# Low parts of weights made by adding transfers, S5 column groups in turn, gated parts one head behind

## The chip, the cores and the metric

One core of a Trainium2 chip runs the whole program. The metric is device time in microseconds for one execution. Three runs of the kernel before took 1574.0 to 1582.47 us, with a median of 1578.91 us. The page and the trace are of one profiled execution, which took 1579.79 us; its span, from the first to the last instruction, is 1577.7 us, so 2.1 us lie outside the span.

The engines by their names in the rows: PE is TensorE (PEld its weight loads), DVE VectorE, ACT ScalarE, POOL GpSimd, SP SyncE, which issues most transfers. GpSimd issues the others, among them those that add to what stands at the target.

## What is computed

A backbone of two layers over 1280 tokens (256 of context, 1024 latent) and 1024 channels. Layer 0 is the one that the change touches: a projection of the normed tokens, a gated linear recurrence (RG-LRU) of 8 heads in both directions, a diagonal state space model (S5) of 32 groups in both directions with a gated linear unit (GLU) behind it, a SiLU gate on each branch, and an output projection. Layer 1 is latent attention of 8 heads. Cut to layer 0:

```python
def rglru_coeffs(u, wr, br, wi, bi, lam):
    r = sigmoid(einsum('blhi,hij->blhj', uh, wr) + br)
    i = sigmoid(einsum('blhi,hij->blhj', uh, wi) + bi)
    log_a = -LRU_C * r * softplus(-lam)
    return exp(log_a), sqrt(-expm1(2.0 * log_a)) * (i * u)      # a, b of h = a h + b

def even_mix(h, ...):
    xa, ga, ub, gb = split(h @ w_in, EVEN_SPLITS, axis=-1)
    ya = rglru_mix(xa, ...)                                      # both directions, added
    yb = s5_mix(ub, ...)                                         # gelu(y) * sigmoid(gelu(y) @ glu_w + glu_b)
    return concatenate([ya * silu(ga), yb * silu(gb)], -1) @ w_out
```

## The kernel before

**High and low parts.** TensorE multiplies in a format shorter than fp32 (fp32r). To keep fp32's precision each operand is held as a rounded high part and the remainder as a low part, and each product is made of three matmuls (`mm3`, L209 to L211): high weight by high data, high weight by low data, low weight by high data. The parts of a weight are made by `split` (L178): ScalarE casts the raw tile to the high part (L182), VectorE subtracts it from the raw tile for the low part (L184). The parts of data are made in the same way by `split_big` (ScalarE L1196, VectorE L1198).

**Buffers.** Raw weights come to SBUF by `raw_weights` (L194, on SyncE's queue) into one buffer of the pool `wp`; high and low parts have two buffers each. Gate weights have two buffers of each kind in the pool `gw`.

**Order.** Layer 0's recurrences are issued in an order written out by hand. Three strings of turns (`TURNS`) name steps; turn n runs with one string, and a step's last character says how many heads it is behind. Turns 0 and 1 run with the first string (they also make the S5 weights, step E), turns 2 to 6 with the second, turn 7 with the third, which runs on into the GLU and the first tiles of the output projection. Each engine executes its instructions in this order and waits only for data and buffers. The second string, and the end of the third:

```python
    ("D01 H11 M11 k21 U1- Q11 a21 G000 l00 N01 P0 G100 s21 B11 r21 U0- d21 D11 N11 W0 P0 o21 l10 a00 "
     "k00 s00 P0 r00 d00 C1- W0 Y1 P0 G110 o00 k10 G010 a10 C0- s10 M00 V0- V1- C2- A10 r10 A00 H00 I- Q00 "
     "d10 P0 O- l20 P0 B00 o10").split(),
     "N00 X10 Z30 N10 J00 X00 X20 F30 X30 P0 Y0 P0 P0 S10 P0 S30 P0 F00 W0 P0 S00 K00 F50 S50 J10 P0 "
     "F40 F20 W0 P0 P0 S40 F70 K10 W0 J20 P0 P0 S20 P0 S70 P0 J30 P0 P0 K20 T10 W0 P0 T00 K30 P0 "
     "P0 F60 T20 W0 S60 T30").split())
```

The steps that matter here:
- U loads a raw gate weight (128x2x128), V makes its parts, G multiplies with it (four times per head, ScalarE's sigmoid at L917 behind each block).
- W makes the parts of the next weight tile and issues the load of the one after it; P multiplies one of the three token blocks (256, 512, 512 columns) of the current tile. The tiles in order: projections of gates and heads, 4 of the GLU (512 rows), 16 of the output projection (768 rows each).
- N are the scans of a head (L943, L947, L948); the first direction's result is stored by GpSimd (L945), the second one's is added to it in DRAM by an adding transfer of GpSimd (Y, L953).
- l, k, a, s, r, d, o are the steps of an S5 batch. In r VectorE scans (L1020, L1021), GpSimd sets two edges to zero (L1023, L1024), VectorE copies (L1025). In d VectorE makes the product that o's matmul L1040 reads.
- E is one step of `s5_weights`, which makes 8 K blocks: for each of four groups, matmuls of 128 columns (L526) and of 16 (L529) into 32 partitions of one PSUM bank; ScalarE copies the bank (L530), VectorE adds the skip term (L531).
- Z, X load and split the S5 output; F loads a head's mixed result and its gate, S multiplies them (L1136) and splits the product at once; K and T do the same for the S5 part with the GLU's result.

`store` sends finished rows from SyncE, in the order in which they were noted, at the next P, E, Z, F or o. `out0` runs the rest of the output projection: six P and two W for each pair of tiles, with `residual` (its store by GpSimd, L1230) behind every second tile.

Of the kernel before, what the change touches and what calls it, by code (L numbers as in the profile page):

```python
# [9 lines left out]
F32 = mybir.dt.float32  # L10
F32R = mybir.dt.float32r
AF = mybir.ActivationFunctionType
ALU = mybir.AluOpType
# [119 lines left out]
class Kernel:  # L133
# [63 lines left out]
    def weight_parts(self, raw):  # L197
        return self.split(raw, self.wp, "w", 2, list(raw.shape))

# [259 lines left out]
    def s5_weights(self, Pre, Pim, bb, ccp):  # L459
# [9 lines left out]
        for Q in range(8):  # L469
            gs = slice(4 * Q, 4 * Q + 4)  # L470
            if Q % 4 == 0:

                Kt = self.tl(sp, [128, 4, 144], "s5K", 1)
                pads = []
# [46 lines left out]
            for g4 in range(4):  # L521
                g = 4 * Q + g4
                o = pk[32 * g4:32 * g4 + 32]
                for k in range(2):
                    C = Cs[k][:, g4].rearrange("p m h -> p (m h)")
                    nc.tensor.matmul(o[:, 16:144], pads[k][:, g % 16], C[:, 16:144], start=(k == 0), stop=(k == 1))  # L526
                for k in range(2):
                    both = bb[:, k, g:g + 2].rearrange("p g h -> p (g h)")
                    nc.tensor.matmul(o[:, 0:16], both, Cs[k][:, g4, 0], start=(k == 0), stop=(k == 1))  # L529
# [358 lines left out]
    def recurrences(self, steps):  # L888
# [8 lines left out]
        class Head:  # L897
# [8 lines left out]
            def V(x, d):  # L906
                x.gw[d] = self.split(x.raw.pop(d), self.gp, "gw", 2, [128, 2, 128])
# [150 lines left out]
        class Tiles:  # L1058
# [3 lines left out]
            def load(x):  # L1062
                if x.n_raw < len(tiles):
                    kind, i, _ = tiles[x.n_raw]
                    src, k = {"glu": (t["glu_w"], 4), "out": (t["w_out"], 6)}.get(kind, (t["w_in"], 8))
                    src = src[i // 2, :, 6 * (i % 2):6 * (i % 2) + 6] if kind == "out" else src[i]
                    x.raws.append(self.raw_weights(src, k))
                    x.n_raw += 1

            def W(x):  # L1070
                if x.raws:
                    x.ws.append(self.weight_parts(x.raws.pop(0)))
                    x.load()

            def P(x):
# [7 lines left out]
                w = x.ws[0]  # L1083
                src = {"glu": lambda: x.y, "out": lambda: self.mix[6 * (i % 2):6 * (i % 2) + 6]}.get(kind, lambda: self.n0)()
# [24 lines left out]
            yg, y, g, gb, m, ga = {}, [None] * 4, {}, {}, {}, {}  # L1109
# [24 lines left out]
            def S(x, h):  # L1134
                m, g = x.m.pop(h), x.ga.pop(h)
                nc.vector.tensor_mul(m, m, g)  # L1136
                self.mix[h] = self.split_big(m, alloc=self.far)
# [697 lines left out]
```

## Time and profile before

| | before |
|---|---|
| median of 3 runs | 1578.91 us (1574.0 to 1582.47) |
| profiled execution | 1579.79 us, span 1577.7 us |
| busy in the span: TensorE, VectorE, ScalarE, GpSimd | 94%, 72%, 52%, 3% |
| transfers: SyncE's queue, GpSimd's queue (share of the 16 engines) | 32.3%, 7.6% |

The page divides the span into 40 slices of 39.4 us. A digit is the busy share of the slice in tenths, one line for each engine. Layer 0's recurrences lie between about 158 and 645 us, its output projection between 645 and 810 us, then come layer 1's projections and the attention. A busy share says nothing of who waits for whom: for that the trace has the waits (who stood idle until whose instruction), the chain of work that ended last, followed back from the end, and the order of instructions in time.

### The profile page before, as it was taken

Reading aid. Unit: us, or ns where it says so; the run is one execution under the profiler, and the core shown is the slowest. Engines: PE = TensorE matmul, PEld = TensorE weight load, DVE = VectorE, ACT = ScalarE, POOL = GpSimd, SP = SyncE. Lnnn points to the kernel's source line nnn. Section 1 sums busy time; section 2 is a strip of 40 time slices with the busy share of each in tenths; the row PEclk is TensorE's granted clock in tenths of the full one; section 3 lists DMA queues with packets and bytes.
Section 4 is the critical chain, followed back from the end, with each engine's and each line's share of the span. In section 5 each row is a group of like instructions: output and inputs, shape, how many; then the busy total and the mean of one; then the engine's idle time right before and its main releaser. Section 6 shows DMA issues by size and latency. Waiting matters only on the chain.

```text
span 1577.7 us, 22599 instructions
## 1 busy us (share of the span) xinstructions
PE 1486.9 (94%) x8690; PEld 1277.5 (81%) x8690; DVE 1138.1 (72%) x1856; ACT 828.3 (52%) x1424; POOL 46.8 (3%) x107
## 2 busy tenths in 40 slices
PE   7899898988988996999999999999999999999997
PEld 4677777877777785878788999888999999999887
DVE  7678788999999888422255625558888888889655
ACT  7457766766866684110143414446555565566532
POOL 0001000000000000000000000010000000000000
PEclk9999999999999998999999999999999999999999
DMA  9355444644655555645351231451120120122353
GB/s 353 135 182 182 163 145 143 180 143 132 193 142 157 167 194 201 230 167 180 134 217 54 81 93 34 152 188 44 31 66 26 64 58 18 40 94 87 105 175 114
DMA packets 96154, 207.76 MB, mean 132 GB/s; under 512 B 9904, under 2 KB 42416, under 8 KB 96048
## 3 DMA queue, kind: packets, MB, share of 16 engines
q1 hardware_dynamic: 86528, 166.65, 32.3%
q0 software_dynamic: 9520, 39.69, 7.6%
q8 instruction: 68, 1.11, 0.3%
q14 instruction: 38, 0.31, 0.1%
HBM read 143.03 MB, written 63.28 MB: 131 GB/s over the span
## 4 chain that ended last, share of the span: by engine, by line
PE 35%; issue 26%; DVE 11%; DMA 2%; ACT 1%; POOL 1%; SPq 0%; DVEq 0%; POOLq 0%; ACTq 0%
PE pv L1580 7%; PE pt L1567 4%; PE S L209 2%; PE S L211 2%; PE S L210 2%; PE S L1519 2%; PE S L1518 2%; PE S L1517 2%; PE S L1516 2%; PE S L1515 2%; DVE H L1020 1%; PE mm L211 1%; PE mm L209 1%; PE mm L210 1%; PE pt L210 1%
## 5 line engine op out<-in xcount | busy, mean ns | idle before, releaser
L182 ACT CAST w_hi<-wraw 128x1024 fp32r<-128x1024 f32 (+3 forms) x73 | 63.3, 867 | 182.6 <-PE mm L210 130.5
L209 PE MATMUL mm<-n0hi,w_hi 128*128 128x512 f32 (+1 forms) x432 | 156.8, 363 | 0.0
L210 PE MATMUL mm<-n0lo,w_hi 128*128 128x512 f32 (+1 forms) x432 | 154.7, 358 | 0.0
L211 PE MATMUL mm<-n0hi,w_lo 128*128 128x512 f32 (+1 forms) x432 | 153.9, 356 | 0.0
L1571 ACT CAST ph<-pt 128x512 fp32r<-128x512 f32 x160 | 91.0, 590 | 83.2 <-PE pt L1567 82.9
L1574 DVE TENSOR_TENSOR pl<-pt,ph 128x512 fp32r<-128x512 f32 x160 | 109.5, 686 | 19.7 <-ACT ph L1571 17.7
L209 PE MATMUL mm<-hi,w_hi 128*128 128x512 f32 (+1 forms) x264 | 100.4, 380 | 11.5 <-ACT w_hi L182 9.5
L209 PE MATMUL mm<-n1hi,w_hi 128*128 128x342 f32 (+2 forms) x336 | 109.6, 329 | 1.7 <-DVE pr L1323 1.7
L210 PE MATMUL mm<-n1lo,w_hi 128*128 128x342 f32 (+2 forms) x336 | 110.2, 328 | 0.0
L211 PE MATMUL mm<-n1hi,w_lo 128*128 128x342 f32 (+2 forms) x336 | 110.1, 328 | 0.0
L1580 PE MATMUL pv<-ph,v 128*128 128x256 f32 x640 | 107.4, 298 | 0.0
L211 PE MATMUL mm<-hi,w_lo 128*128 128x512 f32 (+1 forms) x264 | 98.9, 378 | 5.1 <-DVE w_lo L184 5.1
L210 PE MATMUL mm<-lo,w_hi 128*128 128x512 f32 (+1 forms) x264 | 98.9, 375 | 0.1
L209 PEld LDWEIGHTS mm<-n0hi,w_hi 128*128 128x128 f32 x432 | 82.0, 190 | 12.8
L211 PEld LDWEIGHTS mm<-n0hi,w_lo 128*128 128x128 f32 x432 | 81.7, 189 | 12.7
L210 PEld LDWEIGHTS mm<-n0lo,w_hi 128*128 128x128 f32 x432 | 81.9, 190 | 12.1
L1567 PE MATMUL pt<-c_ident,P 128*128 128x128 f32 x640 | 90.9, 272 | 0.6 <-DVE kl L1497 0.6
L184 DVE TENSOR_TENSOR w_lo<-wraw,w_hi 128x1024 fp32r<-128x1024 f32 (+3 forms) x73 | 72.3, 991 | 25.9 <-ACT w_hi L182 24.9
L1552 ACT ACTIVATE P<-S,sm 128x512 f32<-128x512 f32 x128 | 86.8, 689 | 0.0
L1580 PEld LDWEIGHTS pv<-ph,v 128*128 128x128 f32 x640 | 84.3, 190 | 0.2
L1567 PEld LDWEIGHTS pt<-c_ident,P 128*128 128x128 f32 x640 | 75.7, 140 | 10.4 <-DVE kl L1497 0.8
L1544 DVE TENSOR_REDUCE sm<-S 128x1 f32<-128x512 f32 x128 | 82.0, 680 | 0.8 <-PE S L1519 0.8
(424 smaller groups left out, 4013.9 us busy)
## 6 DMA issues: line engine op xcount, KB each, us to landing
mw<-in_mod_w SPq DMA_DIRECT2D x48, 512.0 KB
wraw<-in_w_in SPq DMA_DIRECT2D x24, 512.0 KB
mixdr<-r POOLq DMA_DIRECT2D x14, 640.0 KB, 5.9
s5wt<-s5scr SPq DMA_DIRECT2D x16, 512.0 KB
ph<-phdr SPq DMA_DIRECT2D x16, 480.0 KB
wraw<-in_mla_in SPq DMA_DIRECT2D x14, 512.0 KB
wraw<-in_w_out SPq DMA_DIRECT2D x16, 384.0 KB
xT<-in_xT SPq DMA_DIRECT2D x8, 640.0 KB
```

The costliest lines, as they stand in the source:

```text
L182: nc.scalar.copy(hi, raw)
L184: nc.vector.tensor_sub(lo, raw, hi.bitcast(F32))
L209: mm(out, w[0], x[0], start=start, stop=False)
L210: mm(out, w[0], x[1], start=False, stop=False)
L211: mm(out, w[1], x[0], start=False, stop=stop)
L1515: mm(d, q[0][:, qs], k[0][:, ks], start=True, stop=False)
L1544: nc.vector.reduce_max(x.sm[e][:, n:n + 1], x.S[e][n], axis=mybir.AxisListType.X)
L1552: nc.scalar.activation(x.P[e][:, s:s + z], x.S[e][n], AF.Exp, bias=sm[:, 4:5], scale=SCALE, accum_out=sm[:, 5 + n:6 + n])
L1567: nc.tensor.transpose(pt[:, i, e], x.P[e][:, key:key + 128], self.ident)
L1571: nc.scalar.copy(x.hi[t], x.pt[t])
L1574: nc.vector.tensor_sub(x.lo[t], x.pt[t], x.hi[t].bitcast(F32))
L1580: mm(x.pv, v[:, 128 * (h % 2):128 * (h % 2) + 128], p, start=x.left == 30, stop=x.left == 1)
```

## The change

Three things, all in layer 0:
1. A new function `split_from` makes the parts of the gate weights (V) and of the tiles of W. ScalarE casts the raw tile to the high part as before, then multiplies the high part by -1 into the low part's tile; a transfer issued by GpSimd then adds the weight, read once more from DRAM, onto it. VectorE has no part in it. The first weight tiles, made before the recurrences, and those of layer 1 are made as before.
2. In the K blocks the loops are exchanged: each kind of matmul goes over the four groups, that is over four sets of 32 columns of TensorE, before the next one of the same group.
3. S multiplies a head's result by its gate and notes it; the parts of the head noted before are made there, one head late. Where a tile of the output projection needs parts that are not made yet, P makes them first.

```diff
--- before.py
+++ after.py
@@ -197,6 +197,16 @@
     def weight_parts(self, raw):
         return self.split(raw, self.wp, "w", 2, list(raw.shape))
 
+    def split_from(self, raw, src, pool, tag):
+
+        nc = self.nc
+        self.n += 1
+        hi, lo = (pool.tile(list(raw.shape), F32R, name=f"{tag}_{n}_{self.n}", tag=tag + n[0], bufs=2) for n in ("hi", "lo"))
+        nc.scalar.copy(hi, raw)
+        nc.scalar.mul(lo, hi.bitcast(F32), -1.0)
+        nc.gpsimd.dma_start(lo, src.bitcast(F32R), accum_op=ALU.add)
+        return hi, lo
+
     def raw_uk(self, h):
         return self.raw_weights(self.t["w_uk"][h], 2)
 
@@ -518,15 +528,17 @@
                 yield
             Cs = [C for C, _ in Cs]
             pk = self.bank([128, 144], "s5", 2)
-            for g4 in range(4):
-                g = 4 * Q + g4
-                o = pk[32 * g4:32 * g4 + 32]
-                for k in range(2):
+
+            for k in range(2):
+                for g4 in range(4):
                     C = Cs[k][:, g4].rearrange("p m h -> p (m h)")
-                    nc.tensor.matmul(o[:, 16:144], pads[k][:, g % 16], C[:, 16:144], start=(k == 0), stop=(k == 1))
-                for k in range(2):
+                    nc.tensor.matmul(pk[32 * g4:32 * g4 + 32, 16:144], pads[k][:, (4 * Q + g4) % 16], C[:, 16:144],
+                                     start=(k == 0), stop=(k == 1))
+            for k in range(2):
+                for g4 in range(4):
+                    g = 4 * Q + g4
                     both = bb[:, k, g:g + 2].rearrange("p g h -> p (g h)")
-                    nc.tensor.matmul(o[:, 0:16], both, Cs[k][:, g4, 0], start=(k == 0), stop=(k == 1))
+                    nc.tensor.matmul(pk[32 * g4:32 * g4 + 32, 0:16], both, Cs[k][:, g4, 0], start=(k == 0), stop=(k == 1))
             nc.scalar.copy(Kt[:, Q % 4], pk)
             stt(Kt[:, Q % 4, 0:16], self.dmask, self.s5d[:, Q:Q + 1], Kt[:, Q % 4, 0:16], ALU.mult, ALU.add)
             if Q % 4 == 3:
@@ -904,7 +916,7 @@
                 nc.sync.dma_start(x.raw[d], self.t["gate_w"][x.h, :, 2 * d:2 * d + 2])
 
             def V(x, d):
-                x.gw[d] = self.split(x.raw.pop(d), self.gp, "gw", 2, [128, 2, 128])
+                x.gw[d] = self.split_from(x.raw.pop(d), self.t["gate_w"][x.h, :, 2 * d:2 * d + 2], self.gp, "gw")
 
             def G(x, d, q):
 
@@ -1064,12 +1076,12 @@
                     kind, i, _ = tiles[x.n_raw]
                     src, k = {"glu": (t["glu_w"], 4), "out": (t["w_out"], 6)}.get(kind, (t["w_in"], 8))
                     src = src[i // 2, :, 6 * (i % 2):6 * (i % 2) + 6] if kind == "out" else src[i]
-                    x.raws.append(self.raw_weights(src, k))
+                    x.raws.append((self.raw_weights(src, k), src))
                     x.n_raw += 1
 
             def W(x):
                 if x.raws:
-                    x.ws.append(self.weight_parts(x.raws.pop(0)))
+                    x.ws.append(self.split_from(*x.raws.pop(0), self.wp, "w"))
                     x.load()
 
             def P(x):
@@ -1081,6 +1093,8 @@
                 b = x.b
                 s, z = BLK[b]
                 w = x.ws[0]
+                if kind == "out" and None in self.mix[6 * (i % 2):6 * (i % 2) + 6]:
+                    x.parts()
                 src = {"glu": lambda: x.y, "out": lambda: self.mix[6 * (i % 2):6 * (i % 2) + 6]}.get(kind, lambda: self.n0)()
                 if kind != "out" or i % 2 == 0:
                     x.ps[b] = self.bank([128, z], "g" if kind == "out" and i % 4 else "mm", 3)
@@ -1106,7 +1120,7 @@
                     x.ws.pop(0)
 
 
-            yg, y, g, gb, m, ga = {}, [None] * 4, {}, {}, {}, {}
+            yg, y, g, gb, m, ga, due = {}, [None] * 4, {}, {}, {}, {}, []
 
             def Z(x, i):
                 self.store()
@@ -1132,9 +1146,16 @@
                 nc.sync.dma_start(x.ga[h], self.gadr[h])
 
             def S(x, h):
+
                 m, g = x.m.pop(h), x.ga.pop(h)
                 nc.vector.tensor_mul(m, m, g)
-                self.mix[h] = self.split_big(m, alloc=self.far)
+                x.parts()
+                x.due.append((h, m))
+
+            def parts(x):
+                while x.due:
+                    h, m = x.due.pop()
+                    self.mix[h] = self.split_big(m, alloc=self.far)
 
             def J(x, i):
                 x.gb[i] = self.big(name="gb")
```

## Rows read from the trace of the kernel before

**Rows 1.** Stages (turns 0, 1, 2, 4, output projection): us, busy by engine, clock, DMA.
```profile
166.00:223.48 57.48, 52.29 (x352) 42.76 (x351) 45.09 (x71) 37.19 (x52) 0.99 (x2) 0.98 0.46 142
223.48:278.43 54.95, 49.77 (x328) 41.62 (x329) 50.91 (x68) 36.67 (x47) 1.45 (x2) 0.93 0.48 141
278.43:323.09 44.66, 43.71 (x239) 37.99 (x238) 41.05 (x45) 33.61 (x46) 1.80 (x6) 0.98 0.63 185
373.90:424.71 50.81, 44.83 (x242) 38.01 (x242) 49.45 (x57) 35.90 (x49) 2.01 (x8) 1.00 0.51 153
...
656.00:804.00 148.00, 148.00 (x814) 118.43 (x814) 37.49 (x57) 18.11 (x20) 3.19 (x6) 1.00 0.50 175
```
**Rows 2.** Waits (total us, times, longest): TensorE 373.9 to 475.5, VectorE 166 to 276.
```profile
PE s L1040 <- DVE G L1033: 9.4, 6, 2.1
...
DVE s5K L531 <- ACT s5K L530: 14.2, 5, 5.6
```
**Rows 3.** VectorE in order of time, turn 5: start us, us, instruction.
```profile
442.38 1.20 DVE L184 TENSOR_TENSOR w_lo<-wraw,w_hi 128x1024 fp32r<-128x1024 f32 x1
443.50 0.48 DVE L1009 TENSOR_TENSOR t<-ph,s 128x320 f32<-128x320 f32 x1
...
461.14 0.76 DVE L184 TENSOR_TENSOR gw_lo<-gwraw,gw_hi 128x256 fp32r<-128x256 f32 x2
```
**Rows 4.** ScalarE in order of time: weight casts, a GLU activation, a T cast.
```profile
189.19 1.05 ACT L182 CAST w_hi<-wraw 128x1024 fp32r<-128x1024 f32 x1
...
431.04 1.10 ACT L182 CAST w_hi<-wraw 128x1024 fp32r<-128x1024 f32 x1
...
605.57 0.60 ACT L182 CAST w_hi<-wraw 128x512 fp32r<-128x512 f32 x1
606.07 1.27 ACT L1100 ACTIVATE glu<-mm,c_gains 128x512 f32<-128x512 f32 x2
...
624.88 1.27 ACT L1196 CAST hi<-gb 128x1280 fp32r<-128x1280 f32 x1
...
656.32 0.81 ACT L182 CAST w_hi<-wraw 128x768 fp32r<-128x768 f32 x1
```
**Rows 5.** GpSimd's transfers of 640 KB by line: L953 (adding), then L945 (plain).
```profile
DMA to landing us min/median/max: 5.8/6.2/6.7
...
DMA to landing us min/median/max: 3.2/3.3/6.5
```
**Rows 6.** TensorE in order of time: the first matmul of four tiles.
```profile
195.47 0.36 PE L209 MATMUL mm<-n0hi,w_hi 128*128 128x256 f32 x1
...
446.35 0.28 PE L209 MATMUL mm<-n0hi,w_hi 128*128 128x256 f32 x1
...
606.22 0.58 PE L209 MATMUL mm<-hi,w_hi 128*128 128x256 f32 x1 [4.82 <-ACT w_hi L182]
...
667.58 0.28 PE L209 MATMUL g<-hi,w_hi 128*128 128x256 f32 x1
```
**Rows 7.** Busy PE and PEld of one line: L526 in a K block, then L276.
```profile
174.80:177.20 2.40, 2.02 (x16) 1.42 (x16) 1.00 0.69 191
...
37.70:38.85 1.15, 1.06 (x8) 0.16 (x8) 1.00 1.05 397
```
**Rows 8.** The chain that ended last, turn 7: start us, us, what.
```profile
537.30 1.24 DVE w_lo L184
...
569.84 0.61 DVE w_lo L184
```
**Rows 9.** Waits from 575 to 645 us, of ScalarE, VectorE and TensorE.
```profile
ACT hi L1196 <- DVE mixa L1136: 17.8, 6, 7.0
...
DVE lo L1198 <- ACT hi L1196: 10.6, 8, 1.3
...
PE mm L209 <- ACT w_hi L182: 8.9, 3, 4.8
PE mm L211 <- DVE w_lo L184: 5.1, 4, 3.8
```

## The prediction

> **What bounds the kernel now.** I read the 40 slices of the page first: TensorE is at 9 tenths almost everywhere, and the only long stretch in which another engine is as full is the recurrences (158 to 645 us), VectorE at 8 or 9. The change touches only that stretch and the output projection behind it, so I cut these by turns [rows 1]. In the middle of the recurrences a turn takes 50.81 us, and VectorE is busy for 49.45 of them (97%), TensorE for 44.83, ScalarE for 35.90. TensorE's waits in two such turns name VectorE's product for 9.4 us [rows 2]: VectorE sets these turns. In turns 0 and 1 nobody is full (TensorE 91% in both, VectorE 78% and 93%): they hand work to each other, and VectorE's one large wait there is 14.2 us in 5 pieces for ScalarE's copy of the S5 K block [rows 2], which TensorE feeds. Turn 2 is TensorE's (43.71 of 44.66). In the output projection TensorE is busy for all of 148.00 us [rows 1]: VectorE work saved there is worth nothing.
>
> **Steady turns (3 to 6).** Each has two weight tiles (128x1024) and two gate tiles (128x256). Their low parts are VectorE subtractions: 1.20 us for a weight, with the next instruction 1.12 us behind its start, and 0.76 us for the two gate tiles together, so 0.68 by the same overlap [rows 3]. Removed: 2 x 1.12 + 0.68 = 2.9 us a turn, on the engine that sets the turn. Added on ScalarE: a multiplication by -1 for each. No such instruction is in the trace. The cast of the same weight took 1.05 to 1.10 us [rows 4]; for a gate tile I take 0.4. That is 2.9 us on an engine with 15 us free in a turn. Added on GpSimd's queue: four transfers that add. Behind them stand the pairs of small memsets that VectorE waits for inside each S5 batch, and the two transfers of the scans. Before the change ScalarE casts the first weight at 431.04 [rows 4] and VectorE subtracts at 442.38 [rows 3]: ScalarE runs 10 us ahead, so its multiplications should be done before GpSimd comes to them. I cost the queue at nothing; without that lead each late multiplication would hold VectorE by up to its own 0.4 to 1.1 us.
> Does the low part come in time? The nearest row is the adding transfer of 640 KB that the kernel already has (L953): 5.8 to 6.7 us from issue to landing, median 6.2, against a median of 3.3 for a plain one of that size (L945) [rows 5]. A smaller one should lie between 6.2 (size doesn't matter) and 6.2 x size/640. I take the middle: 5.6 us for 512 KB, 5.0 for 384, 4.4 for 256; for the range, the plain 3.3 below and 6.7 above. The first weight of a turn could be issued at 433.2 (its cast's end plus 1.05); 2 us later, behind memsets, it still lands near 441, and TensorE starts on that tile at 446.35 [rows 6]. Covered by 5 us.
> What is late next: TensorE's 44.83 us, which leave it 3 us of waits in a turn of 47.9 where it had 6. They are mostly for VectorE and shrink with it, but not wholly. I take 2.6 of the 2.9 us: 4 x 2.6 = **-10.5 us** (-12 to -6).
>
> **Turns 0 to 2.** The K block (8 of them, in turns 0 and 1) makes four 32-column groups one after the other: 16 matmul instructions of 128 columns take 2.02 us, about 0.5 a group. Where the kernel already takes the groups in turn (L276), 8 instructions of 512 columns take 1.06 us [rows 7]: twice the columns in half the time, so four run at once. The block, with its 16-column ones, should go from some 2.1 to 0.6 us: 8 x 1.45 = 11.6 us off TensorE, most of it where VectorE waited. VectorE also loses 2 x 2.9 us. Against it stands one weight in each of the two turns that is needed soon: cast at 189.19 for a tile used at 195.47 [rows 4, 6]. Two gate multiplications ahead of it (0.4 each counts once, the other runs before), its own 1.05 and 5.6 us to land make it about 2 us late; twice, 4 us of the gain. Turn 2, TensorE's, gives about 1. Bounds: VectorE's side lets the two turns shrink by 5.8 + 5 x 1.45 = 13; none of it, with two low parts late and partly hidden, is +2. I take half of 13 and turn 2's 1: **-7 us** (-14 to +2).
>
> **Turn 7, first part.** In the chain of waits two subtractions, at 537.30 and at 569.84, stand ahead of SyncE's queue [rows 8]: the next raw tile is loaded into the buffer that they read, and the stores behind that load (gate rows, S5 outputs) wait too. After the change only the cast reads the raw tile. It was done before the subtraction began, so the queue moves at least 1.24 and 0.61 us earlier, more by the time that the subtraction stood in VectorE's queue. The new multiplications (1.05 and 0.6) stand ahead of ScalarE's next activations. I take **-3 us** (-6 to 0).
>
> **Turn 7, gated parts and GLU.** Now ScalarE's cast of a gated head waits for VectorE's product of the same head (17.8 us in all), VectorE then waits for that cast (10.6 us), and the weight casts queue behind both: TensorE waits 8.9 us for casts and 5.1 us for low parts [rows 9], 4.82 of it at 606.22 [rows 6]. One head behind, the cast has its input long before: VectorE's 10.6 us go, and a weight cast moves up to the end of the block whose activation stands ahead of it. But these weights are needed at once, and each now has a multiplication and a landing behind its cast. TensorE's wait by tile, with activation 0.7, GLU cast 0.6, T cast 1.3, output cast 0.8 [rows 4], and a block of 12 matmuls at some 2.7 us (the projection has 814 in 148.00 us, 0.18 each, the wide ones more [rows 1]): GLU tile 1, 0.7 + 0.6 + 0.6 + 4.4 less one block, 3.6; tile 2, less two blocks, 0.9; tile 3, none; first output tile, whose cast stands behind the last activation and a T cast, 0.7 + 1.3 + 0.8 + 0.8 + 5.0 = 8.6. The sum is 13.1 against 14.0 now. Activations that no longer queue behind a waiting cast give about 1 more: **-2 us** (-8 with landings near 3.3, +5 with 6.7 and casts that don't move up).
>
> **Output projection.** 15 more weights go the new way. The cast at 656.32 feeds the tile that starts at 667.58 [rows 4, 6]; behind it and a multiplication of 0.8 there are 9.6 us for a landing of 5.0. Ahead in GpSimd's queue is only the store of a finished tile. Zero; +4 if a few land late.
>
> **Sum**: -10.5 - 7 - 3 - 2 = -22.5. The profiled execution took 1579.8 us (span 1577.7), 0.9 over the median of the runs, so both bases give 1557 within a microsecond.
>
> The plain transfer's row is 3.3 us for 640 KB; no row prices an add into SBUF. The Trainium skill (DMA: Bandwidth & Descriptors, section Anatomy of one DMA — SWDGE) gives about 2.0 us plus bytes over 436 GB/s, an estimate of 3.5 us for 640 KB: the plain row agrees, the adding row (6.2) doesn't. By that rule 512 KB would land in 3.2 us and the five tight places below would gain some 10 us more, for 1547.
>
> **The rivals.**
> (a) TensorE takes over. It has 88% of a steady turn already, and ScalarE, for which it also waits, gets 2.9 us more work: turns 3 to 6 give 1 us each, turns 0 to 2 only 2, the rest as above: -11, **1569**. For it: TensorE's 91% and 98% in turns 0 to 2. Against it: its waits in the steady turns name VectorE.
> (b) Slower: the adds into SBUF land late. Five places have no slack (one weight each in turns 0 and 1, GLU tiles 1 and 2, the first output tile), so each further microsecond of landing costs 5. At about 10 us the gain is gone; over 9.6 us the 15 output tiles stall too. At 12 us: 5 x 6.4 = +32 and 15 x 2.4 = +36 against -22.5, **1625**. For it: an adding transfer lands 2.9 us later than a plain one, and none in the trace adds into SBUF. Against it: seven adds of 640 KB beside full traffic never took over 6.7 us.
> (c) Landings of 9 to 10 us, or adds that hold the memsets behind them in GpSimd's queue for 1 us in each of a turn's three batches and lose what VectorE gained: **1578**.
> (d) The column groups don't overlap, so the change doesn't do there what it says: turns 0 to 2 give -1 instead of -7, **1563**. The row of L276 speaks against it.
>
> **How the numbers follow.** Forecast 0.60, (a) 0.14, (b) 0.10, (c) 0.12, (d) 0.04. Predicted 1557. The forecast's own bounds run from -40 to +5, but not all ends come together: 1539 is near the lower one. Upwards the range reaches over (d) and (a) to the edge of (c): 1575. Half a per cent is 7.9 us, about what a measurement can tell from no change. Faster: forecast, (d) and 0.12 of (a), 0.76; same: (c) and the rest of (a), 0.14; slower: (b), 0.10.
>
> **What would show it.** Steady turns of about 48.2 us with VectorE still over 95% busy, or of 50 with TensorE at 90% (a). Landings of the new transfers of 4 to 6 us, or 10 and more (b, c). K blocks of 0.6 us. In the GLU, TensorE's waits on the landing of w_lo instead of on VectorE and ScalarE. The prediction is wrong if TensorE waits for landings in the steady turns or in the output projection, or if GpSimd's memsets come late to VectorE.

## The result, and the profile after

The changed kernel takes 1590.16 us (median of 6 runs, 1588.70 to 1594.07) against 1579.19 for the kernel before on the same chip: ratio 1.008, interval 1.006 to 1.010. The forecast was 1557, in a range of 1539 to 1575. So the change makes the kernel slower, by 33 us more than I thought, and the time lies outside the range.

To see where the 12.8 us of the two spans lie (1577.7 before, 1590.5 after), I cut both traces at the same instructions: the first scan of a turn (N01), and the first and last store of the residual. Differences in us:

| stage | forecast | measured |
|---|---|---|
| turns 0 to 2 (from 118 us) | -7 | +6.4 |
| turns 3 to 5 | -7.8 | -0.2 |
| turn 6 | -2.6 | -1.9 |
| turn 7, first part | -3 | -4.0 |
| turn 7, gated parts, GLU, first output tile | -2 | +11.1 |
| output projection | 0 | +1.3 |
| rest | 0 | -0.1 |

The first view is busy time by stage, as in [rows 1]: turns 0, 1, 2, 4 and the output projection of the changed kernel (us of the stretch, busy by engine with counts, granted clock, DMA share, GB/s).

```profile
166.00:225.51 59.51, 48.05 (x352) 39.18 (x350) 42.83 (x70) 39.98 (x56) 4.38 (x6) 0.93 0.62 169
225.51:284.51 59.00, 47.90 (x326) 39.52 (x327) 48.15 (x64) 39.27 (x51) 4.81 (x6) 0.85 0.58 154
284.51:329.52 45.01, 43.94 (x239) 37.66 (x237) 38.12 (x41) 36.26 (x50) 5.26 (x10) 0.99 0.75 205
380.29:431.03 50.74, 46.52 (x243) 39.79 (x242) 46.60 (x53) 38.47 (x53) 5.45 (x12) 0.97 0.66 176
...
668.00:816.00 148.00, 146.97 (x807) 117.58 (x807) 26.61 (x44) 28.66 (x32) 14.39 (x19) 1.00 0.72 210
```

In the fourth row VectorE has lost just what was taken from it, 49.45 to 46.60, and yet the turn takes 50.74 instead of 50.81: it is not VectorE that sets it now. TensorE's busy time rose by 1.7 us with the same work; the granted clock, 1.00 before, is 0.97. In turns 0 and 1 nobody is full, as before, and TensorE has gone from 91% to 81%.

Whom does TensorE wait for? First turns 0 and 1 (166 to 285 us), with VectorE's row that answers to the K block's in [rows 2]; then the gated parts, GLU and first output tile (570 to 668 us), which answer to [rows 9] (total us, times, longest).

```profile
PE mm L221 <- DMA w_lo<-in_w_in: 9.6, 2, 5.1
...
DVE s5K L543 <- ACT s5K L542: 26.5, 7, 8.4
ACT row L1109 <- PE mm L221: 19.8, 5, 6.1
```
```profile
PE mm L221 <- DMA w_lo<-in_glu_w: 12.4, 3, 5.6
...
PE mm L221 <- DMA w_lo<-in_w_out: 8.5, 1, 8.5
...
ACT w_hi L205 <- DMA wraw<-in_glu_w: 5.6, 1, 5.6
DVE lo L1219 <- ACT hi L1217: 10.5, 4, 6.2
```

Every wait of TensorE of more than 3 us in these stretches is now for the landing of a low part: 9.6 us in all, and 20.9 us. Before, TensorE waited 14.0 us for casts and low parts together in the second [rows 9]. VectorE's wait for the K block did not go either: 14.2 us [rows 2] became 26.5. ScalarE's copy of the block stands behind a row activation, which waits for the matmuls (L221) that wait for the low part.

The low parts' transfers by kind (KB of one, median us from issue to landing), which answer to [rows 5]:

```profile
w_lo<-in_w_in POOLq DMA_DIRECT2D x17, 512.0 KB, 6.3
...
w_lo<-in_w_out POOLq DMA_DIRECT2D x16, 384.0 KB, 7.3
...
gw_lo<-in_gate_w POOLq DMA_DIRECT2D x16, 128.0 KB, 6.6
...
w_lo<-in_glu_w POOLq DMA_DIRECT2D x4, 256.0 KB, 5.7
```

These medians do not follow size: 128 KB lands no sooner than 512. But they mix places with different traffic. The first gate weight of turns 0 and 1, with no transfer of GpSimd's just ahead of it, landed after 3.0 and 3.1 us; in turns 2 to 6, issued among SyncE's loads for the next S5 batch, the same 128 KB took 6.5 to 7.1 us. And transfers issued close together land one behind the other. In turn 0 two gate weights and the weight that is needed at 193.29 are issued at 187.96, 188.9 and 190.91 and land after 3.0, 5.5 and 7.9 us, the last at 198.8. The landings in two windows, of the two gate weights and of the weight, and below them those of the transfers of L965 (L953 before, where they took 5.8 to 6.7 us [rows 5]), which are now issued 0.5 us behind a weight's low part:

```profile
DMA to landing us min/median/max: 3.0/4.2/5.5
...
DMA to landing us min/median/max: 7.9/7.9/7.9
...
DMA to landing us min/median/max: 8.2/9.1/11.4
```

TensorE has stood still since the two products that need no low part, and goes on at half speed:

```profile
193.29 0.36 PE L219 MATMUL mm<-n0hi,w_hi 128*128 128x256 f32 x1
193.49 0.28 PE L220 MATMUL mm<-n0lo,w_hi 128*128 128x256 f32 x1
198.88 0.58 PE L221 MATMUL mm<-n0hi,w_lo 128*128 128x256 f32 x1 [5.12 <-DMA w_lo<-in_w_in]
```

The steady turn shows two places. TensorE waits 1.94 us for VectorE's product, and 0.7 us after that wait it falls to the half clock (1.2 of 2.4 GHz): the eight products of L1013, 1.49 us at full clock, take 2.22. Later VectorE waits 2.78 us for the next batch's products. In order of time, TensorE, with the window that shows its clock (0.50), then ScalarE, then VectorE:

```profile
393.57 0.54 PE L1052 MATMUL s<-G,s5wt 128*128 128x160 f32 x2 [1.94 <-DVE G L1045]
...
395.74 2.22 PE L1013 MATMUL s<-U,s5wt 128*128 128x160 f32 x8
```
```profile
394.30:397.70 3.40, 3.40 (x16) 3.40 (x14) 3.33 (x3) 1.44 (x3) 0.00 (x0) 0.50 0.74 135
```
```profile
404.71 1.05 ACT L205 CAST w_hi<-wraw 128x1024 fp32r<-128x1024 f32 x1
405.79 1.06 ACT L206 ACTIVATE w_lo<-w_hi 128x1024 fp32r<-128x1024 f32 x1
406.87 1.28 ACT L1109 ACT_TABLE_LOAD   x1
408.16 0.39 ACT L1109 ACTIVATE row<-mm 128x256 f32<-128x256 f32 x1
408.56 1.28 ACT L929 ACT_TABLE_LOAD   x1
409.86 1.63 ACT L929 ACTIVATE i<-g,c_lru 128x256 f32<-128x256 f32 x3
```
```profile
413.19 0.49 DVE L1021 TENSOR_TENSOR t<-ph,s 128x320 f32<-128x320 f32 x1 [2.78 <-PE s L1013]
```

ScalarE has 12 us free in this turn, but none here: from 404.0 to 411.5 one instruction follows the other, and the sigmoids at 409.86, which release TensorE's gate products and through them the S5 products, come behind the new multiplication.

### The profile page after: what moved, and what is told of

Read it like the earlier page. It is cut to its first block, busy times and chain, and to the rows that moved or that the text cites. A ratio compares the mean times of both kernels' runs of the same rounds, so it can differ in the third digit from the quotient of the medians.

```text
span 1590.5 us, 22716 instructions
## 1 busy us (share of the span) xinstructions
PE 1487.2 (94%) x8690; PEld 1278.4 (80%) x8690; DVE 1098.2 (69%) x1803; ACT 865.9 (54%) x1477; POOL 92.1 (6%) x160
## 4 chain that ended last, share of the span: by engine, by line
PE 49%; issue 22%; DVE 11%; DMA 3%; ACT 3%; POOL 1%; SPq 0%; POOLq 0%; DVEq 0%; ACTq 0%
PE pv L1601 7%; PE pt L1588 4%; PE mm L221 4%; PE mm L219 4%; PE mm L220 4%; PE S L219 2%; PE S L221 2%; PE S L220 2%; PE S L1540 2%; PE S L1537 2%; PE S L1538 2%; PE S L1539 2%; PE S L1536 2%; DMA w_lo<-in_w_out 1%; DVE H L1032 1%
## 5 line engine op out<-in xcount | busy, mean ns | idle before, releaser
L221 PE MATMUL mm<-n0hi,w_lo 128*128 128x512 f32 (+1 forms) x432 | 156.2, 361 | 9.6 <-DMA w_lo<-in_w_in 9.6
L1595 DVE TENSOR_TENSOR pl<-pt,ph 128x512 fp32r<-128x512 f32 x160 | 109.5, 687 | 19.7 <-ACT ph L1592 17.8
L221 PE MATMUL mm<-hi,w_lo 128*128 128x512 f32 (+1 forms) x264 | 99.8, 381 | 20.9 <-DMA w_lo<-in_glu_w 12.4
L221 PE MATMUL mm<-n1hi,w_lo 128*128 128x342 f32 (+2 forms) x336 | 110.4, 329 | 0.0
L221 PEld LDWEIGHTS mm<-n0hi,w_lo 128*128 128x128 f32 x432 | 83.7, 194 | 22.8 <-DMA w_lo<-in_w_in 10.0
L182 ACT CAST w_hi<-wraw 128x1024 fp32r<-128x1024 f32 (+3 forms) x36 | 29.6, 822 | 110.6 <-PE mm L220 99.0
L221 PEld LDWEIGHTS mm<-hi,w_lo 128*128 128x128 f32 x264 | 52.3, 198 | 31.6 <-DMA w_lo<-in_glu_w 13.0
```

Source lines behind the costliest of these rows:

```text
L221: mm(out, w[1], x[0], start=False, stop=stop)
L1595: nc.vector.tensor_sub(x.lo[t], x.pt[t], x.hi[t].bitcast(F32))
```

## The experiments

All stages of all kernels in one table, cut as above (without the rest): us more (+) or less (-) than before, each from one profiled execution; behind them the ratio of the times to the kernel before, with its interval.

| kernel | turns 0-2 | 3-5 | 6 | 7, first | GLU to first tile | output | ratio (95%) |
|---|---|---|---|---|---|---|---|
| changed | +6.4 | -0.2 | -1.9 | -4.0 | +11.1 | +1.3 | 1.008 (1.006, 1.010) |
| x1_groups | -4.8 | 0 | 0 | -0.5 | +0.3 | 0 | 0.995 (0.994, 0.997) |
| x2_behind | -1.8 | 0 | 0 | -0.1 | -0.5 | 0 | 0.999 (0.998, 1.000) |
| x3_adds | +2.9 | -3.0 | -0.4 | -3.9 | +11.2 | +1.8 | 1.008 (1.006, 1.011) |
| x4_slack | -5.6 | -1.4 | -0.4 | -3.4 | -1.3 | 0 | 0.993 (0.992, 0.995) |
| x5_plain | -5.1 | -1.6 | -0.4 | -3.9 | +7.4 | 0 | 1.000 (0.999, 1.001) |
| x6_nomul | -4.2 | -5.2 | -2.4 | -4.0 | -2.6 | 0 | 0.991 (0.988, 0.993) |
| x9_spare | -0.3 | -2.3 | -1.6 | -2.9 | -0.8 | 0 | 0.996 (0.995, 0.998) |
| x8_noadd | -6.6 | 0 | +1.4 | -0.5 | +1.1 | 0 | 0.995 (0.994, 0.997) |
| x7_second | -5.2 | -4.8 | -1.5 | -3.0 | +2.7 | 0 | 0.991 (0.988, 0.994) |
| x10_fill | -0.3 | -1.3 | -0.8 | -0.7 | +13.9 | +1.0 | 1.009 (1.007, 1.011) |
| x11_fill6 | +2.2 | -4.5 | -1.8 | -2.3 | +13.2 | +0.7 | 1.003 (1.002, 1.005) |
| x12_second_fill6 | -4.1 | -5.4 | -2.1 | -2.9 | -2.5 | 0 | 0.988 (0.984, 0.991) |

How far a single number may be trusted is in the table too: x10 and x11 carry out the same instructions in turns 0 to 2 as the changed kernel, and stand at -0.3 and +2.2 where that one stands at +6.4. TensorE's waits for landings in these turns differ likewise: 9.6 us in the changed kernel, 7.4 in x10, 7.2 in x11. So a few us in that column tell nothing. The same holds for the GLU's: x4, x7, x8 and x12 make its low parts alike, on VectorE, and stand between -2.5 and +2.7. The turns 3 to 5 of one kernel differ by 0.1 us at most where the granted clock is the same (0.3 in x4).

**The three parts alone.** x1_groups: the kernel before with the K block's loops exchanged, and nothing else.

> The kernel before with the exchanged loops of the K blocks alone. Theory A (the exchanged loops are a gain, the time is lost where low parts land late): K blocks of 0.7 us instead of 2.1, turns 0 and 1 together 5 to 10 us shorter, 1570 to 1574 us. Theory B (the K blocks are not on the path, turns 0 and 1 are set by VectorE or ScalarE): no change, 1577 to 1581 us.

x2_behind: the kernel before with the gated parts one head behind.

```diff
                 nc.vector.tensor_mul(m, m, g)
-                self.mix[h] = self.split_big(m, alloc=self.far)
+                x.parts()
+                x.due.append((h, m))
...
```

> The kernel before with the gated parts one head behind, and nothing else. Theory A: VectorE's 10.6 us of waits for ScalarE's casts in turn 7 go and TensorE starts the output projection earlier, 1570 to 1576 us. Theory B (a head's product holds its buffer until its parts are made one head later, so loads into those buffers come later and SyncE's queue with them): VectorE's waits for loaded gates rise from 0.3 to over 5 us, 1582 to 1588 us.

x3_adds: the kernel before with the low parts by multiplication and adding transfer, K block and gated parts as before.

```diff
-                x.gw[d] = self.split(x.raw.pop(d), self.gp, "gw", 2, [128, 2, 128])
+                x.gw[d] = self.split_from(x.raw.pop(d), self.t["gate_w"][x.h, :, 2 * d:2 * d + 2], self.gp, "gw")
...
-                    x.ws.append(self.weight_parts(x.raws.pop(0)))
+                    x.ws.append(self.split_from(*x.raws.pop(0), self.wp, "w"))
```

> The kernel before with the low parts made by adding transfers, and nothing else. Theory A (landings): TensorE waits for landings in turns 0 and 1 (10 us), in the GLU and at the first output tile (20 us), partly beside waits of before, 1590 to 1600 us, slower than the whole change. Theory B (the harm is in the gated parts one head behind): 1574 to 1580 us.

The exchanged loops gain 0.5% by themselves, all in turns 0 to 2 (-4.8). The gated parts one head behind can't be told from nothing. The low parts alone give the whole loss, 1.008, and the same +11 us in the GLU. So the loss is the low parts', and the exchanged loops don't reach the result beside them.

Why they don't is seen in turns 0 and 1 of x3_adds: TensorE's wait for the landings, and the landing of turn 0's weight.

```profile
PE mm L221 <- DMA w_lo<-in_w_in: 3.8, 2, 2.0
...
DMA to landing us min/median/max: 5.3/5.3/5.3
```

The adding transfers and SyncE's load beside them are those of the changed kernel. But with the old loops the two gate weights go out 1.7 us apart (3.1 in turn 1) instead of 0.9, and the weight behind them lands after 5.3 us (5.4) instead of 7.9 (7.4); in x10 and x11, again 0.9 apart, it takes 5.7 to 7.0. So the exchanged loops also push the adding transfers together. That this makes them land late is read from these traces; no run changes the spacing alone.

What x2_behind's waits show from 573 to 643 us (total us, times, longest) is where its gain goes:

```profile
ACT w_hi L182 <- DMA wraw<-in_glu_w: 11.4, 1, 11.4
...
ACT hi L1204 <- DVE mixa L1138: 4.5, 3, 1.6
```

ScalarE's wait for the product went from 17.8 us [rows 9] to 4.5 as meant, and the weight's cast behind it then waits 11.4 us for the raw tile, whose load stands in SyncE's queue behind the loads of the gated rows. VectorE waits 5.7 us for those rows (0.3 before), as the second theory had it, but the time does not rise; 1577.6 us lies between the two theories.

**Low parts back to VectorE where there is no slack.** x4_slack is the changed kernel with VectorE's subtraction for the weights of turns 0 and 1, of the GLU and of the output projection; the rest stays with the adding transfers.

```diff
-                    x.ws.append(self.split_from(*x.raws.pop(0), self.wp, "w"))
+                    raw, src, kind = x.raws.pop(0)
+                    if x.turn < 2 or kind in ("glu", "out"):
+                        x.ws.append(self.weight_parts(raw))
+                    else:
+                        x.ws.append(self.split_from(raw, src, self.wp, "w"))
...
```

> The changed kernel, but the weights of W made in turns 0 and 1 and all of the GLU and of the output projection have their low part from VectorE again; the adding transfers stay for the gate weights and for the weight tiles made in turns 2 to 7 for projections. Theory A: no wait for a landing is left, the gain of the K blocks and of turn 7 stays, the steady turns stay at 50.7 us: 1564 to 1572 us. Theory B (gated parts one head behind): turn 7's GLU stays long, 1578 to 1586 us.

12.1 us come back in turns 0 to 2 and 12.4 in the GLU, and the kernel is faster than both (0.993). The tight places are where the time went.

x8_noadd has no adding transfer at all: the exchanged loops and the gated parts one head behind, low parts by VectorE.

> The changed kernel with all low parts by VectorE again: only the exchanged K-block loops and the gated parts one head behind are left. Theory A (the two parts add up): 1579.3 - 8.7 - 1.7 = 1569, with turns 0 to 2 at -5 and the GLU within 1 us of before. Rival: the gated parts are worth more or less beside the fast K blocks: 1565 or 1573. Against x4_slack (1567.4) it tells what the adds in slack places bring: by the stages of x4_slack 1.5 us in one steady turn and 4 us in turn 7, so x8_noadd should be 3 to 6 us above it.

0.995, as x1_groups alone. Against x4_slack it shows what the adds bring in places with slack: some 3 us in the first part of turn 7, and little in the steady turns.

**Which part of a low part's way costs?** Three kernels in which the time alone is read. x5_plain makes the adding transfer a plain one of the same bytes; x6_nomul also leaves out ScalarE's multiplication, so that the transfer needn't wait for anything but its buffer; x9_spare has the multiplication again, into a tile that nobody reads.

```diff
         nc.scalar.copy(hi, raw)
         nc.scalar.mul(lo, hi.bitcast(F32), -1.0)
-        nc.gpsimd.dma_start(lo, src.bitcast(F32R), accum_op=ALU.add)
+        nc.gpsimd.dma_start(lo, src.bitcast(F32R))
```
```diff
-        nc.scalar.mul(lo, hi.bitcast(F32), -1.0)
```
```diff
+        spare = self.wp.tile([128, 4, 128], mybir.dt.bfloat16, name=f"spare_{self.n}", tag="spare", bufs=1)
+        for k in range(0, raw.shape[1], 4):
+            e = min(4, raw.shape[1] - k)
+            nc.scalar.mul(spare[:, :e], hi[:, k:k + e].bitcast(F32), -1.0)
```

> The changed kernel with its adding transfers made plain ones of the same bytes (no adding; so the low part is the whole weight, a part of the computation that is changed, and only the time is read). ScalarE's multiplication stays. Theory A (the landing of 6 to 7 us is what the tight places pay): a plain transfer lands about 3 us sooner; turns 0 to 2 shrink by 5 to 8 us, the stretch from the GLU to the first output tile by about 9 us (three waits of 5.6, 5.0 and 8.5 us, 3 each), the steady turns stay at 50.7; in all 1573 to 1578. Theory B (ScalarE's multiplications in its queue are what is paid, the landing is not): within 3 us of the changed kernel, 1587 to 1593. If the plain transfer lands as late as the adding one (6 to 7 us), adding is not what makes the landing late, and the time stays too.

> As x5_plain, and without ScalarE's multiplication too, so that the low part's transfer waits for nothing but its buffer (the low part is the whole weight: only the time is read). Theory A: turns 0 to 2 at or below those of x1_groups (5 us less than before the change), the GLU 2 to 5 us less than before the change, and in the steady turns, where ScalarE's multiplication of the second weight lies on the way to the gate's sigmoids, 48.5 to 49.5 us a turn instead of 50.7; in all 1553 to 1562. If the multiplication doesn't matter there, the steady turns stay at 50.7 and the whole at 1563 or more.

> As x6_nomul (the low part is a plain load of the weight, so only the time is read), but ScalarE multiplies all the same, into a spare tile that nobody reads (in pieces of at most 512 columns, some 0.2 us more for a weight of 1024). So ScalarE's queue carries what it carries in the changed kernel, and the low part waits neither for it nor for a landing behind it. Theory A (in the GLU the low part's place behind cast, multiplication and landing is what costs; in the steady turns ScalarE's multiplication itself): the GLU stretch near x6_nomul's (1 us under before, 9 us under x5_plain), the steady turns back at 50.7 or 49.3 as in x5_plain; in all 1563 to 1568. Rival: ScalarE's queue is what costs in the GLU too: the stretch stays 6 to 10 us over before, in all 1572 or more.

Landings in x5_plain (KB, median us), the same kinds as above but for the third:

```profile
w_lo<-in_w_in POOLq DMA_DIRECT2D x17, 512.0 KB, 5.0
w_lo<-in_w_out POOLq DMA_DIRECT2D x16, 384.0 KB, 5.4
...
w_lo<-in_glu_w POOLq DMA_DIRECT2D x4, 256.0 KB, 4.8
```

By the medians adding is worth 0.9 to 1.9 us of a landing; the rest, 5 us, a plain transfer costs too. I had expected 3 us less and got 1 to 2. But the weights of turns 0 and 1 that are needed at once, behind the same gate weights, land after 3.9 us both times instead of 7.9 and 7.4. So there adding, one transfer close behind another, is worth 4 us. Here is turn 0's:

```profile
DMA to landing us min/median/max: 3.9/3.9/3.9
```

In turns 0 and 1 TensorE's waits for landings fall from 9.6 us to 2.2, and turns 0 to 2 by 11.5. In the GLU only 3.7 of the 11.1 us come back, where 9 were expected: TensorE still waits 16.6 us for landings there.

```profile
PE mm L221 <- DMA w_lo<-in_glu_w: 10.2, 2, 6.4
PE mm L221 <- DMA w_lo<-in_w_out: 6.4, 1, 6.4
```

x9_spare settles what these are. ScalarE's queue is as long as in the changed kernel, the low part is early, TensorE waits for no landing, and the GLU stands at -0.8. So it is not ScalarE's multiplication as work that costs there (the rival falls): it is that the landing comes after cast and multiplication of a weight that is needed at once. The stage decides this, not the total: 1574.87 us is in the rival's range, since turns 0 to 2 stand at -0.3. x6_nomul's 1563.72 us is over its range too, though its stages are near those expected.

**The steady turns.** There x6_nomul, whose low parts cost neither VectorE nor ScalarE anything, takes 48.8 us a turn, and x9_spare 49.6, both where the clock stays full. Two turns of one kernel, x3_adds, show the other part (the first window is 0.1 us wider than its turn, which takes 50.73 us):

```profile
375.30:426.10 50.80, 46.57 (x243) 39.70 (x242) 46.67 (x54) 38.55 (x53) 5.45 (x12) 0.97 0.66 179
426.10:475.40 49.30, 45.34 (x242) 38.15 (x242) 46.59 (x54) 38.45 (x53) 5.42 (x12) 1.00 0.67 184
```

The same work takes 50.73 us with a half-clock stretch (clock 0.97) and 49.31 without. To make this an experiment, x10_fill repeats the first product of the S5 output batch 12 times where TensorE waits 1.9 us; x11_fill6 repeats it 6 times. Both are the changed kernel otherwise.

```diff
+                for _ in range(6 if x.b % 3 == 2 else 0):
+                    nc.tensor.matmul(p[:, 0], x.w[:, 4, 0], x.U[:, 0], start=True, stop=True)
                 for g in range(2):
                     nc.tensor.matmul(p[:, g], x.w[:, 4, g], x.U[:, g], start=True, stop=False)
...
```

> The changed kernel with 12 more matrix instructions (each 160 columns, the first product of the S5 output batch repeated, whose result the real one writes over) put where TensorE waits 1.9 us for VectorE's product once in each of turns 3 to 7, ahead of the stretch at the half clock. Theory A (the half clock that follows this wait costs each steady turn 1.5 us): the granted clock stays at full speed in the three steady turns and each falls from 50.7 to about 49.3; in all 1584 to 1587. Rival (the half clock costs nothing there, since VectorE or ScalarE sets the turn anyway, and the repeats stand in TensorE's way): 50.7 to 51.5 a turn, 1590 to 1594.

> As x10_fill with 6 repeats in place of 12. There the 12 took 3.25 us (each is two instructions of 0.136 us), 1.06 longer than the wait that they were to fill, and the steady turns, now at full clock, fell by 0.43 only. Theory A (the half clock is worth 1.5 us a turn, and the filling that stood over took 1.06 of it): 6 repeats end inside the wait, the clock stays at full speed and the steady turns take 49.3 us; in all some 5 us below the changed kernel, 1584 to 1587. Rival (the half clock is worth only some 0.4 to 0.7 us there): 50.0 to 50.4 a turn. Third: 6 repeats leave 0.5 us of the wait, and the half clock comes back: 50.7.

With 12 the half-clock stretches of the steady turns were gone, but a turn took 50.38 and the whole 1593.89 us, as the rival had it: I had counted each repeat as one instruction of 0.14 us, and it is two, so the repeats stood 1.06 us in TensorE's way. With 6 they end inside the wait. TensorE in order of time, and the whole turn:

```profile
385.54 1.79 PE L1051 MATMUL s<-U,s5wt 128*128 128x160 f32 x12
...
387.92 0.54 PE L1054 MATMUL s<-G,s5wt 128*128 128x160 f32 x2 [0.32 <-DVE G L1045]
...
389.39 1.49 PE L1013 MATMUL s<-U,s5wt 128*128 128x160 f32 x8
```
```profile
374.60:424.00 49.40, 47.06 (x255) 39.80 (x254) 46.68 (x54) 38.55 (x53) 5.45 (x12) 1.00 0.66 183
```

(The window is 0.1 us wider than the turn.) L1013's eight products take 1.49 us instead of 2.22, and turns 3 to 5 take 1.45, 1.42 and 1.41 us less than in the changed kernel. The half clock costs 1.4 us a steady turn. That the repeats keep it away, and not chance, rests on counts: in the three kernels with repeats none of the twelve turns 3 to 6 has a half-clock stretch, in the seven without repeats whose low parts come by transfers of GpSimd, 15 of 28 have one. It costs nothing where VectorE sets the turn. Here is a steady turn of x8_noadd, at the half clock for a while too, with VectorE at 49.44:

```profile
367.40:418.20 50.80, 46.27 (x242) 39.68 (x241) 49.44 (x58) 35.66 (x49) 2.01 (x8) 0.97 0.50 150
```

x7_second is x4_slack with the second weight of each turn, the one whose multiplication stands ahead of the sigmoids, given back to VectorE; x12_second_fill6 is that with the 6 repeats.

```diff
                     raw, src, kind = x.raws.pop(0)
-                    if x.turn < 2 or kind in ("glu", "out"):
+                    x.odd = not x.odd
+                    if x.turn < 2 or x.odd or kind in ("glu", "out"):
```

> As x4_slack, but in turns 2 to 7 the second weight of a turn gets its low part from VectorE again, the first one and the gate weights by adding. Theory A (ScalarE's multiplication of the second weight holds the gates' sigmoids and by them TensorE and VectorE): the steady turns fall from 50.7 to 49 to 50, in all 1561 to 1565. Rival: VectorE's busy time still sets the turns, so 1.1 us a turn more on it lengthens them: 1568 to 1572. Third: neither, the loop has no room for either, 1566 to 1568.

> x7_second with the 6 repeats: low parts in turns 0 and 1, of the GLU, of the output projection and of the second weight of a turn by VectorE, the rest by adding. Two of x7_second's steady turns had a half-clock stretch behind this wait (from 381 and from 480 us); Theory A: these two fall by about 1 us each, the others stay, in all 1562 to 1564 or no difference that can be told from x7_second's ratio 0.991. Rival: the repeats cost: 1566 or more.

x7_second's turns at full clock take 49.0, 0.3 less than x11_fill6's although VectorE has 1.1 us more to do: VectorE doesn't set x11_fill6's turn, the way through ScalarE does. VectorE's wait for the S5 products shows by how much. Here it is in one turn of the changed kernel, of x11_fill6 and of x6_nomul, and then a turn of x7_second, where there is no such wait:

```profile
DVE t L1021 <- PE s L1013: 2.8, 1, 2.8
...
DVE t L1021 <- PE s L1013: 1.4, 1, 1.4
...
DVE t L1020 <- PE s L1012: 0.8, 1, 0.8
```
```profile
317.89:366.89 49.00, 44.95 (x244) 38.19 (x243) 47.65 (x54) 37.83 (x52) 4.57 (x11) 1.00 0.66 180
```

Before the change a turn was 1.36 us longer than VectorE's busy time (50.81 and 49.45). Busy time, 1.36 and this wait give all four turns to 0.1 us: 46.6 + 1.36 + 2.8 = 50.8, with 1.4 it is 49.4, with 0.8 it is 48.8, and 47.65 + 1.36 = 49.0. So in x7_second VectorE sets the turn again, as before the change.

x12_second_fill6 has three turns of 49.0 and takes 1559.87 us (median of 4), ratio 0.988: the lowest of all and faster than both kernels, though its interval meets x7_second's. Its span is 7.0 us shorter than x7_second's, but only 0.6 of that lies in turns 3 to 5 and 0.6 in turn 6; 5.2 lie in the GLU, whose instructions are the same, and these I can't explain.

## Why the prediction was wrong, step by step

The forecast was -22.5 us and the spans differ by +12.8. Three steps hold nearly all of the 35 us between: turns 0 to 2 with their two late weights (13.4), the GLU with the first output tile (13.1) and the steady turns 3 to 5 (7.6).

**K blocks: right in the duration, a little high on the path.** Forecast 0.6 us for a block, measured 0.69 (175.85 to 176.54) against some 2.1 [rows 7]. I took half of 13 us for turns 0 and 1; x1_groups gave 4.8 with turn 2.

**Two late weights: mis-sized, and this is the step that turned turns 0 to 2.** I counted each as 2 us late by a landing of 5.6. The landings were 7.9 and 7.4 us, since I let the gate weights' multiplications stand ahead of them but not their transfers, which landed ahead of them too. Apart from one another they cost what I said: in x3_adds the landings are 5.3 and 5.4 us and TensorE waits 3.8 us for the two. The exchanged loops, which I added up as a gain of their own, push them together. In the changed kernel TensorE waited 9.6 us for the two, not 4, and ran at the half clock for much more of the stretch: from 118 us to the end of turn 2 the mean granted clock is 0.91 over 211.5 us, before 0.96 over 205.1. I had left the clock out of the sum. x5_plain, with landings of 2.3 to 5.8 us in turns 0 and 1 against 3.0 to 7.9, gets all of it back. x3_adds without the exchanged loops loses 2.9, x1_groups without adds gains 4.8, and both together should give -1.9; the three executions gave -0.3, +2.2 and +6.4. How much of that excess is the later landings, how much the clock and how much ScalarE's queue was not separated: x9_spare, with early low parts and the multiplications, stands at -0.3, and x6_nomul without them at -4.2, which is inside the scatter of this stage.

**Steady turns: the relief was right, the bound behind it was not.** VectorE lost 2.85 us a turn (2.9 forecast). I let 2.6 of it through, since TensorE's waits were for VectorE and ScalarE had 15 us free. Three things took it. The loop through TensorE and ScalarE lets only 2.0 through at full clock with no multiplication (x6_nomul, 48.8). The multiplications take back 0.5 (x11_fill6, 49.3), the second weight's at least 0.3 (x7_second, 49.0): "an engine with 15 us free" was an average, and at that place it has none. And the half clock takes the last 1.4. So -2.0 + 0.5 + 1.4 = -0.1, as measured. No landing was late in these turns and GpSimd's memsets made VectorE wait 0.6 us as before: these two steps were right. Rival (a) named the first two causes and priced them at 1 us a turn left; nobody named the third. Why the half clock fell into the changed kernel's turns and not into those of before [rows 1] I can't say in general. Before, TensorE waited 2.1 us at its longest in the same place [rows 2] and stayed at full clock; x8_noadd, whose steady turns have the same instructions, fell to the half clock in each of them.

**Turn 7, first part: right.** Forecast -3, measured -4.0. x3_adds (-3.9) shows that it is the low parts that give it, as the step said.

**Gated parts and GLU: wrong by 13 us.** I forecast waits of 13.1 us against 14.0. By tile, forecast and measured: GLU tile 1 3.6 and 5.6, tile 2 0.9 and 1.7, tile 3 none and 5.0, first output tile 8.6 and 11.2 (2.7 for its cast, 8.5 for the landing): 23.5. Two terms failed. The landings of these three tiles were 5.6 to 6.4 us and 8.2 for the output tile, not 4.4 and 5.0. And the sentence that a weight's cast moves up once the gated casts no longer wait failed for tile 3: its cast waited 5.6 us for the raw tile, whose load stood in SyncE's queue, a queue that I followed for turn 7's first part and not here. VectorE's wait of 10.6 us for the casts [rows 9], which I let go, is 10.5 after.

**Output projection: right but for 1.3 us.** The landings (7.3 us in the median) stayed inside the 9.6 us of cover but for the longest, 9.9 us. For it TensorE waited, which the prediction had named as a sign of being wrong:

```profile
810.75 0.39 PE L221 MATMUL g<-hi,w_lo 128*128 128x256 f32 x1 [1.03 <-DMA w_lo<-in_w_out]
```

**The landings** themselves are the common cause. I took the middle between "size doesn't matter" and "in proportion to size" and got 4.4 to 5.6. For the first weight of turns 3 to 6, with no other transfer issued in the 3 us before it, that was right: 5.3 to 5.6 us for 512 KB. What failed was to give a size one price, without what is issued just ahead of it. My upper end, 6.7, was the longest of seven transfers that were issued apart from each other; the same seven take 8.2 to 11.4 behind a weight's. Rival (b) had the mechanism (adds into SBUF land late, five tight places) with a price of 12 us; it decided at 6 to 8 already: I had set the point from which it decides by gains of 22.5 us, of which the steady turns' part did not come. The Trainium skill's line for a transfer (DMA: Bandwidth & Descriptors, section Anatomy of one DMA — SWDGE: about 2.0 us and bytes over 436 GB/s), by which 512 KB would land in 3.2 us (an estimate from its figures), comes near for plain transfers issued alone: 3.5 to 3.7 us for the first weight of turns 3 to 6 in x5_plain. It is far off for the median of the plain ones, 5.0 us, and for the adding ones, 5.3 to 5.6 alone and 6.3 in the median.

## What to carry to other kernels

Before work is moved off the busiest engine, ask for each place how long the result may take to come, not how free the receiving engine and queue are on the average: the same edit gained 3 us in turn 7's first part, where a low part had time, and lost 11 in the GLU, where it was needed at once, and giving it up in those places alone (x4_slack) made a slower kernel a faster one. Price a landing by the transfers that are issued just ahead of it, and walk every queue that its input stands in, also SyncE's. And when a change takes a bound away, look at what TensorE's new idle stretches do to its clock: there half of what a steady turn could have gained went (1.4 of 2.9 us), and six repeated products brought it back.

## What I had not expected of the hardware

- An adding transfer into SBUF landed after 5.7 to 7.3 us in the median for 128 to 512 KB, in no order of size; plain ones in the same places after 4.8 to 5.4. What was issued just ahead counted more than size or adding: the same 512 KB in turns 0 and 1 landed after 7.9 and 7.4 us with the two adding transfers ahead 0.9 us apart, after 5.3 and 5.4 with them 1.7 and 3.1 apart (x3_adds), and after 3.9 with all three plain (x5_plain).
- After TensorE's wait of 1.94 us in a steady turn its granted clock was 0.50 from 394.3 to 397.7; with 6 repeated products in the wait (0.32 us of it left) it was 1.00 in the whole turn, and the turn 1.4 us shorter. The same half clock cost nothing in a turn that VectorE set (50.82 us with clock 0.97 in x8_noadd, 50.81 with 1.00 before).
- Eight products of 128 columns on four 32-column groups taken in turn, 16 instructions, took 0.65 us, against 2.02 one group after the other [rows 7].
